# A two-layer encoder trunk on one core: expert weights in units of 2048 columns, and a finer alternation of large and small experts

## The chip, the core and the metric

The kernel runs on one core of a Trainium2 chip. The metric is the device time of one execution in microseconds; the median of three runs before the change is 1777.73 us (1777.11 to 1779.68). The engines are TensorE (PE; its weight loads are PEld), VectorE (DVE), ScalarE (ACT), GpSimd (POOL) and SyncE (SP), which issues the DMAs. Each works through its own queue in order.

## The reference

Two layers over 256 tokens of width 1024, all in float32. Each layer runs four token mixers (stick-breaking attention, spatial gating, chunk-band attention, an SSD scan) on one combined input projection, merges them by sigmoid gates, projects, and normalises. Then comes the channel sublayer, a dense SwiGLU in layer 0 and eight experts in layer 1, plus a gated per-layer embedding, and another normalisation:

```python
def swiglu(x, w_gate, w_up, w_down):
    return (jax.nn.silu(x @ w_gate) * (x @ w_up)) @ w_down
...
    top_val, top_idx = lax.top_k(logits, TOP_K)          # 2 of 8 experts a token
    gates = jax.nn.softmax(top_val, axis=-1)
...
    for e in range(N_EXPERTS):
        y = y + combine[..., e:e + 1] * swiglu(x, w_gate[e], w_up[e], w_down[e])
```

An expert has three matrices of 1024 x 3584 float32, 44 MB; all eight are read, 352 MB.

## The kernel before, in words

Weights and activations are used as pairs, `hi` (rounded to the matmul format F32R) and `lo` (the rest). `load` brings one weight unit of 128 rows x 1024 columns (512 KB, 4 KB rows) from HBM into a raw buffer; `split` makes `hi` by a ScalarE cast (L117) and `lo` by a VectorE subtraction (L118). `tmm` (L202) multiplies three passes: hi x hi, x.lo x hi, x.hi x lo, one matmul of 512 columns each.

The expert stage (`moe`) begins with the lead expert, number 7, whose weights need no routing result; the other seven follow in the order of their token counts, at places 1 to 7, their numbers read into registers of SP (L1200). Places 0 to 4 are large (class `Expert`, 128 token slots), places 5 to 7 small (class `Small`, 64 slots). An expert's 3584 inner columns go in seven chunks of 512. A chunk takes four units of gate weights, four of up and four of down: `proj(c, 0)`, `proj(c, 1)`, `turn(c)` (transposes of the hidden chunk on TensorE, into `pht` or `phs`, and a split of the result, `et` or `es`), `down(c)`. A unit costs a large expert six matmuls. A small expert puts hi and lo of its 64 slots side by side as 128 columns of the stationary operand (`passes`, L1057): four matmuls a unit, the upper 64 rows of the result holding the lo share. These halves are added afterwards: ScalarE copies the upper half to `st` (L1075), VectorE adds (L1082 for gate, L1092 for up), then comes the product (L1093).

`steps` (L1205 to L1214) writes the order by hand: three chunks of the first large expert, then the other 32 large chunks with 21 small chunks spread among them, chunk by chunk. Within a step the next chunk's gate projection, this chunk's turn, the next chunk's up projection and this chunk's down projection follow. Small work (SiLU, copies, products, splits) is `Delayed` by a number of loads, `D_SILU`, `D_MULT`, `D_TURN` = 3, 1, 1, and put behind that load's `hi` or `lo` on its engine. Gathers of token rows and the combination of an expert's result with the output are `tasks`, of which `tick` runs one piece after each unit.

Buffers: raw units rotate over 5 + 3 + 8 places, `hi` over five, `lo` over four. PSUM has three `stream` banks (projections, gathers, combines) and five `acc` banks (turns and down sums). While layer 1's embedding gate runs, ten units of the lead expert are loaded ahead (L1343 to L1350).

Of the kernel before, what the change touches and what calls it, by code (L numbers as in the profile page):

```python
# [17 lines left out]
P = 128  # L18
# [7 lines left out]
NE = 8  # L26
# [18 lines left out]
MLATE, MRAW = 3, 11  # L45
SK, TAIL = 4, 7
D_SILU, D_MULT, D_TURN = 3, 1, 1
# [3 lines left out]
ALONE = 3  # L51
# [47 lines left out]
def trunk_kernel(ctx: ExitStack, tc: tile.TileContext, a: dict, out: bass.AP):  # L99
# [5 lines left out]
    ring = ctx.enter_context(tc.tile_pool(name="ring", bufs=1))  # L105
    base = ctx.enter_context(tc.tile_pool(name="base", bufs=2))
    psum = ctx.enter_context(tc.tile_pool(name="psum", bufs=1, space=PSUM))

    def pst(name):
        return psum.tile([P, 512], F32, tag="stream", name=name, bufs=3)  # L110

    def psa(name):
        return psum.tile([P, 512], F32, tag="acc", name=name, bufs=5)
# [7 lines left out]
    spare = []  # L121
    count = [0]

    def raw_unit():

        i = count[0] % (RAW + MRAW)
        count[0] += 1
        if spare and i >= RAW:
            if i >= RAW + MLATE:
                return spare[1].tile([P, UN], F32, tag="mraw", name="mraw", bufs=MRAW - MLATE)  # L130
            return spare[0].tile([P, UN], F32, tag="mraw", name="mraw", bufs=MLATE)
        return ring.tile([P, UW], F32, tag="raw", name="raw", bufs=RAW)

    def load(src, n=UN, keep=None):
# [6 lines left out]
        if keep is None:  # L141
# [103 lines left out]
    sel(tris, -1, -1, 1, 0.0)  # L245
    iota = const.tile([P, P], F32, name="iota")
# [695 lines left out]
    class Weights:  # L942


        def __init__(self, e):
# [5 lines left out]
            self.proj = [[[m[c, i] for i in range(4)] for c in range(NCH)] for m in (g, u)]  # L951
            self.down = [d[k] for k in range(FE // P)]

        def first(self, n):

            g, u = self.proj
            return (g[0] + u[0] + g[1] + u[1] + self.down[0:4] + g[2] + u[2] + self.down[4:8])[:n]

    class Expert:
# [26 lines left out]
        def turn(self, c):  # L986
            self.mult.pop(c)()
            h, ps = self.h.pop(c), psa("pht")
# [13 lines left out]
        def down(self, c):  # L1002
            self.turned()
            if c == 0:
                self.acc = [psa("pey0"), psa("pey1")]
            for j in range(FC // P):
                k = c * (FC // P) + j
                w = load(self.w.down[k])
                x = self.hT[:, j * P : (j + 1) * P]
                ends = k == 0, k == FE // P - 1  # L1010
                tmm(*[(self.acc[h], w[:, h * 512 : (h + 1) * 512], x, *ends) for h in range(2)])
                self.tick()
# [39 lines left out]
    class Small(Expert):  # L1052
# [11 lines left out]
        def proj(self, c, which):  # L1064
            ps = pst("ps" + "gu"[which])
            for u in range(4):
                w = load(self.w.proj[which][c][u]).view("p (k c) -> p k c", k=2)
                ks = 2 * u, 2 * u + 1
                self.passes([(ps, w[:, k % 2, :], self.xg[:, k, :], k == 0, k == KD - 1) for k in ks])
                self.tick()  # L1070
            new = lambda n: self.fp.tile([HS, FC], F32, tag=n, name=n)
            t = new("st")

            def bring():
                after(nc.scalar.copy(t, ps[HS:P, :]), 0)  # L1075

            bring = Delayed(D_MULT, bring)
            if which == 0:
                self.h[c] = g = new("sg")

                def add():
                    after(nc.vector.tensor_tensor(g, ps[0:HS, :], t, op=ALU.add), 1)  # L1082

                add = Delayed(D_MULT + 1, add)
                silu = Delayed(D_SILU, lambda: after(act(g, g, AF.Silu), 0))
                self.silu = lambda: (bring(), add(), silu())
            else:
# [3 lines left out]
                def mult():  # L1091
                    nc.vector.tensor_tensor(t, ps[0:HS, :], t, op=ALU.add)  # L1092
                    nc.vector.tensor_tensor(g, g, t, op=ALU.mult)  # L1093

                mult = Delayed(D_MULT + 1, mult)
                self.mult[c] = lambda: (bring(), mult())

        def turn(self, c):
            self.mult.pop(c)()
            h, ps = self.h.pop(c), psa("phs")  # L1100
            n = FC // P
            for j in range(n):
                nc.tensor.transpose(ps[:, j * HS : (j + 1) * HS], h[:, j * P : (j + 1) * P], ident[:HS, :HS])
# [11 lines left out]
        def down(self, c):  # L1115
            self.turned()
            if c == 0:
                self.acc = [psa("pes0"), psa("pes1")]
            for j in range(FC // P):
                k = c * (FC // P) + j  # L1120
                w = load(self.w.down[k])
                ends = k == 0, k == FE // P - 1
                self.passes([(self.acc[h], w[:, h * 512 : (h + 1) * 512], self.hT[:, j, :], *ends) for h in range(2)])
# [9 lines left out]
    def moe(l, x, xt, fp, ep, route, lead, placed, first, second):  # L1133
# [71 lines left out]
        big = [(p, c) for p in range(BIG) for c in range(NCH)]  # L1205
        small = [(p, c) for p in range(BIG, NE) for c in range(NCH)]
        steps, big = big[:ALONE], big[ALONE:]
        nb, ns = len(big), len(small)
        done = 0
        for i, b in enumerate(big):  # L1210
            steps.append(b)
            while done < (i + 1) * ns // nb:
                steps.append(small[done])
                done += 1  # L1214
        ex = {}

        def expert(p):
            if p not in ex:
                w = lead if p == 0 else Weights(ids[p])
                ex[p] = (Expert if p < BIG else Small)(w, xgs[p], fp, ep, tick)  # L1220
            return ex[p]

        held.extend([None] * 3 + placed * 3)
        expert(0).proj(0, 0)
        tasks.append(prepare_small())
        expert(0).proj(0, 1)
        for n, (p, c) in enumerate(steps):
            if (p, c) == (0, 2):
                route.gates()
            if (p, c) == (0, 4):  # L1230
                list(second)
                tasks.append(prepare_pair(1))
            if (p, c) == (1, 1):
                tasks.append(prepare_pair(3))
            nxt = steps[n + 1] if n + 1 < len(steps) else None
            if nxt:
                expert(nxt[0]).proj(nxt[1], 0)
            ex[p].turn(c)
            if nxt:
                ex[nxt[0]].proj(nxt[1], 1)  # L1240
            ex[p].down(c)
            if c == NCH - 1:
                e = ex.pop(p)
                rank, sel_ = route.rank_at[:, :, p], route.sel_at[:, :, p]
                choice = lambda e=e, r=rank, s=sel_, o=chosen.pop(p, None): e.choice(r, s, o)
                tasks.append(e.combine(choice, route.gate_at[:, :, p], x, nxt is None))
# [26 lines left out]
    for l in range(DEPTH):  # L1273
# [57 lines left out]
        mixctx.close()  # L1331

# [228 lines left out]
```

## Time and profile before

| | |
|---|---|
| median of 3 runs | 1777.73 us |
| profiled execution, its own time | 1778.45 us |
| its span, first to last instruction | 1776.4 us |
| TensorE / VectorE / ScalarE busy | 1698.3 / 1402.4 / 1165.8 us |
| HBM read | 486 MB, 274 GB/s over the span |

Times in a profile are counted from the first instruction. Busy times of different stages are added up in the page, so a stage is read from a window of its own. A matmul's end is modelled, and it is drawn longer than the distance to the next one; the distance between starts is what it costs. A wait is put down to the engine that ended last before it.

### The profile page before, as it was taken

How to read it: one execution, taken by the hardware profiler on the slowest of the kernel's cores; microseconds unless marked ns; L12 is line 12 of the kernel's file. 1: busy time of each engine (PE TensorE's matmuls, PEld its weight loads, DVE VectorE, ACT ScalarE, POOL GpSimd, SP SyncE). 2: the span in 40 equal slices, each digit the busy share in tenths (PEclk: the TensorE clock that was granted, in tenths of full speed). 3: DMA queues.
4: the chain of work that ended last, by engine and by line, in shares of the span. 5: the costliest groups of instructions: out<-in, count | busy, mean ns of one | idle time of the engine just before them, and what ended most of it. 6: DMA issues, size and time to landing. Idle time of an engine off the chain costs nothing.

```text
span 1776.4 us, 27784 instructions
## 1 busy us (share of the span) xinstructions
PE 1698.3 (96%) x9476; PEld 1375.4 (77%) x9476; DVE 1402.4 (79%) x1645; ACT 1165.8 (66%) x1493; POOL 59.8 (3%) x129
## 2 busy tenths in 40 slices
PE   8999999999999999999999999999999999999995
PEld 8989998999899899878776766666666676667663
DVE  7646577455685475879899899999889899999997
ACT  6466445444455564468787878777777777777783
POOL 1000000000010000131000000000000000000001
PEclk9999999999999999999999999999999999999998
DMA  8633566566655358549899999999999999999991
GB/s 296 207 100 118 185 202 212 188 189 181 199 183 154 96 187 275 185 181 351 316 378 359 357 366 380 359 337 370 368 381 338 378 373 352 362 359 372 376 377 73
DMA packets 135862, 489.39 MB, mean 275 GB/s; under 512 B 15392, under 2 KB 15648, under 8 KB 135712
## 3 DMA queue, kind: packets, MB, share of 16 engines
q1 hardware_dynamic: 135712, 487.54, 76.9%
q8 instruction: 76, 1.25, 0.3%
q14 instruction: 74, 0.61, 0.1%
HBM read 486.43 MB, written 1.05 MB: 274 GB/s over the span
## 4 chain that ended last, share of the span: by engine, by line
PE 76%; DVE 9%; DMA 6%; ACT 4%; issue 3%; POOL 2%; DVEq 0%; SPq 0%; ACTq 0%; POOLq 0%
DVE lo L118 6%; PE pey L209 4%; PE peu L209 4%; PE peu L205 4%; PE peu L207 4%; PE peg L209 3%; PE pg L200 3%; PE pg L198 3%; PE pg L197 3%; PE peg L205 3%; PE peg L207 3%; ACT hi L117 3%; PE pey L205 3%; PE pey L207 3%; PE pes L1062 2%
## 5 line engine op out<-in xcount | busy, mean ns | idle before, releaser
L118 DVE TENSOR_TENSOR lo<-raw,hi 128x1024 fp32r<-128x1024 f32 (+1 forms) x444 | 529.4, 1211 | 181.0 <-PE pg L200 75.6
L117 ACT CAST hi<-raw 128x1024 fp32r<-128x1024 f32 (+1 forms) x444 | 455.0, 1044 | 265.3 <-PE pgu L198 49.7
L118 DVE TENSOR_TENSOR lo<-mraw,hi 128x1024 fp32r<-128x1024 f32 x464 | 543.4, 1216 | 23.8 <-ACT hi L117 17.3
L117 ACT CAST hi<-mraw 128x1024 fp32r<-128x1024 f32 x464 | 465.2, 1049 | 44.1 <-PE pey L207 13.6
L197 PE MATMUL pg<-xhi,hi 128*128 128x256 f32 x512 | 125.9, 283 | 0.1
L198 PE MATMUL pg<-xlo,hi 128*128 128x256 f32 x512 | 125.6, 283 | 0.0
L198 PEld LDWEIGHTS pg<-xlo,hi 128*128 128x128 f32 x512 | 97.0, 189 | 1.3 <-issue 1.3
L197 PEld LDWEIGHTS pg<-xhi,hi 128*128 128x128 f32 x512 | 97.0, 189 | 0.5 <-ACT t L697 0.5
L209 PE MATMUL pey<-lo,et 128*128 128x512 f32 x280 | 92.3, 411 | 3.5 <-DVE lo L118 2.6
L205 PE MATMUL pey<-hi,et 128*128 128x512 f32 x280 | 90.1, 402 | 5.8 <-ACT hi L117 5.4
L209 PE MATMUL peg<-lo,xghi 128*128 128x512 f32 x280 | 88.7, 398 | 0.3 <-DVE lo L118 0.2
L205 PE MATMUL peu<-hi,xghi 128*128 128x512 f32 x280 | 88.7, 396 | 0.0
L205 PE MATMUL peg<-hi,xghi 128*128 128x512 f32 x280 | 88.4, 395 | 0.0
L207 PE MATMUL peg<-hi,xglo 128*128 128x512 f32 x280 | 88.0, 393 | 0.0
L207 PE MATMUL pey<-hi,et 128*128 128x512 f32 x280 | 88.0, 395 | 0.0
L209 PE MATMUL peu<-lo,xghi 128*128 128x512 f32 x280 | 87.6, 394 | 0.3 <-DVE lo L118 0.3
L207 PE MATMUL peu<-hi,xglo 128*128 128x512 f32 x280 | 87.4, 393 | 0.0
L198 PE MATMUL pgu<-xlo,hi 128*128 128x256 f32 x352 | 85.9, 282 | 0.0
L197 PE MATMUL pgu<-xhi,hi 128*128 128x256 f32 x352 | 85.8, 282 | 0.0
L200 PE MATMUL pg<-xhi,lo 128*128 128x256 f32 x512 | 78.5, 287 | 0.0
L1062 PE MATMUL psu<-lo,xs 128*64 128x512 f32 x168 | 55.9, 414 | 19.0 <-DVE lo L118 19.0
L205 PEld LDWEIGHTS pey<-hi,et 128*128 128x128 f32 x280 | 50.9, 188 | 25.0 <-ACT hi L117 12.8
(374 smaller groups left out, 3200.0 us busy)
## 6 DMA issues: line engine op xcount, KB each, us to landing
mraw<-in_moe_down SPq DMA_DIRECT2D x156, 512.0 KB, 5.7
mraw<-in_moe_up SPq DMA_DIRECT2D x154, 512.0 KB, 5.8
mraw<-in_moe_gate SPq DMA_DIRECT2D x152, 512.0 KB, 5.3
raw<-in_w_feat SPq DMA_DIRECT2D x104, 512.0 KB, 3.6
raw<-in_moe_gate SPq DMA_DIRECT2D x70, 512.0 KB, 5.3
raw<-in_moe_up SPq DMA_DIRECT2D x70, 512.0 KB, 5.8
raw<-in_moe_down SPq DMA_DIRECT2D x68, 512.0 KB, 6.2
raw<-in_ffn_gate SPq DMA_DIRECT2D x22, 512.0 KB, 3.6
```

What stands on the lines that cost most here:

```text
L117: i = nc.scalar.copy(hi, src)
L118: return i, nc.vector.tensor_tensor(lo, src, hi.bitcast(F32), op=ALU.subtract)
L197: mm(o, w.hi, x.hi, start=first, stop=False, skip_group_check=True)
L198: mm(o, w.hi, x.lo, start=False, stop=False, skip_group_check=True)
L200: mm(o, w.lo, x.hi, start=False, stop=last, skip_group_check=True)
L205: mm(o, x.hi, w.hi, start=first, stop=False, skip_group_check=True)
L207: mm(o, x.lo, w.hi, start=False, stop=False, skip_group_check=True)
L209: mm(o, x.hi, w.lo, start=False, stop=last, skip_group_check=True)
L1062: mm(o[0:HS, :], x[:, 0:HS], w.lo, start=False, stop=last, skip_group_check=True)
```

## The change

Expert units are 2048 columns wide: 1 MB with 8 KB rows, two per projection and two per down chunk, with the HBM layout changed to match (also that of the embedding gate and projection). The narrow ring is closed before layer 1's channel sublayer, and a wide one opened (7 raw, 3 `hi`, 3 `lo`). Large and small experts are two generators that yield after each two units; nine steps of the large ones come first. A small expert's SiLU result is written to both halves of 128 rows, the up result is multiplied unfolded, and the turning matmul uses `ident2`, two 64-column identities on top of each other, so that it adds the halves. PSUM becomes four `stream` banks, two for large and two for small down sums; turns use `stream`. The lead expert's ahead loads are seven wide units, three before the router's and four behind.

```diff
-MLATE, MRAW = 3, 11
+WU = 2048
+WRAW, WLATE, WHI, WLO = 6, 1, 3, 3
 SK, TAIL = 4, 7
-D_SILU, D_MULT, D_TURN = 3, 1, 1
+D_SILU, D_MULT, D_TURN = 2, 2, 1
 LEAD = NE - 1
 BIG = 5
 HS = P // 2
-ALONE = 3
+ALONE = 9
...
+        return psum[0].tile([P, 512], F32, tag="stream", name=name, bufs=few[0])
+
+    def psa(name, tag="acc"):
+        return psum[0].tile([P, 512], F32, tag=tag, name=name, bufs=many[0])
+
+    def other_banks():
+
+        psumctx.close()
+        psum[0] = psumctx.enter_context(tc.tile_pool(name="psume", bufs=1, space=PSUM, reuse_waits="tile"))
+        few[0], many[0] = 4, 2
...
+        return wide_ring[i >= WRAW].tile([P, WU], F32, tag="wraw", name="wraw", bufs=(WRAW, WLATE)[i >= WRAW])
+
+    def begin_load(src):
+
+        raw = raw_unit()
+        nc.sync.dma_start(raw[:, : src.shape[-1]], src)
+        ahead.append((src, raw))
...
+        elif wide_ring:
+            hi = wide_ring[1].tile([P, WU], F32R, tag="hi", name="whi", bufs=WHI)
+            lo = wide_ring[1].tile([P, WU], F32R, tag="lo", name="wlo", bufs=WLO)
...
+    ident2 = const.tile([P, HS], F32, name="ident2")
+    nc.vector.tensor_tensor(ident2, ident[:, 0:HS], ident[:, HS:P], op=ALU.add)
...
-            for u in range(4):
-                w = load(self.w.proj[which][c][u]).view("p (k c) -> p k c", k=2)
-                ks = 2 * u, 2 * u + 1
-                tmm(*[(ps, w[:, k % 2, :], self.xg[:, k, :], k == 0, k == KD - 1) for k in ks])
+            for u in range(2):
+                w = load(self.w.proj[which][c][u], WU).view("p (k c) -> p k c", k=4)
+                ks = range(4 * u, 4 * u + 4)
+                tmm(*[(ps, w[:, k % 4, :], self.xg[:, k, :], k == 0, k == KD - 1) for k in ks])
...
-                self.h[c] = g = new("sg")
-
-                def add():
-                    after(nc.vector.tensor_tensor(g, ps[0:HS, :], t, op=ALU.add), 1)
-
-                add = Delayed(D_MULT + 1, add)
-                silu = Delayed(D_SILU, lambda: after(act(g, g, AF.Silu), 0))
+                g = self.fp.tile([P, FC], F32, tag="sg", name="sg")
+                t = self.fp.tile([HS, FC], F32, tag="st", name="st")
+                self.h[c] = g
+
+                def silu():
+                    for h in (slice(HS, P), slice(0, HS)):
+                        after(act(g[h, :], t, AF.Silu), 0)
+
+                bring = Delayed(D_MULT, lambda: after(nc.scalar.copy(t, ps[HS:P, :]), 0))
+                add = Delayed(
+                    D_MULT + 1, lambda: after(nc.vector.tensor_tensor(t, ps[0:HS, :], t, op=ALU.add), 1)
+                )
+                silu = Delayed(D_SILU + 2, silu)
                 self.silu = lambda: (bring(), add(), silu())
             else:
                 self.silu()
                 g = self.h[c]
 
-                def mult():
-                    nc.vector.tensor_tensor(t, ps[0:HS, :], t, op=ALU.add)
-                    nc.vector.tensor_tensor(g, g, t, op=ALU.mult)
-
-                mult = Delayed(D_MULT + 1, mult)
-                self.mult[c] = lambda: (bring(), mult())
+                self.mult[c] = Delayed(
+                    D_MULT, lambda: after(nc.vector.tensor_tensor(g, g, ps, op=ALU.mult), 1)
+                )
 
         def turn(self, c):
             self.mult.pop(c)()
-            h, ps = self.h.pop(c), psa("phs")
+            h, ps = self.h.pop(c), pst("phs")
             n = FC // P
             for j in range(n):
-                nc.tensor.transpose(ps[:, j * HS : (j + 1) * HS], h[:, j * P : (j + 1) * P], ident[:HS, :HS])
+                m1(ps[:, j * HS : (j + 1) * HS], h[:, j * P : (j + 1) * P], ident2)
...
+            for which in range(2):
+                expert(places[0]).proj(0, which)
+                yield
+            for n, (p, c) in enumerate(steps):
+                if (p, c) == (0, 2):
+                    route.gates()
+                if (p, c) == (0, 4):
+                    list(second)
+                    tasks.append(prepare_pair(1))
+                if (p, c) == (1, 1):
+                    tasks.append(prepare_pair(3))
+                nxt = steps[n + 1] if n + 1 < len(steps) else None
+                if nxt:
+                    expert(nxt[0]).proj(nxt[1], 0)
+                    yield
...
+                ex[p].turn(c)
+                if nxt:
+                    ex[nxt[0]].proj(nxt[1], 1)
+                    yield
+                ex[p].down(c)
...
+        held.extend([None] + placed * 2)
+        tasks.append(prepare_small())
+        big, small = run(range(BIG)), run(range(BIG, NE))
+        nb, ns = BIG * NCH * 3 - ALONE - 3, (NE - BIG) * NCH * 3
+        for i in range(ALONE):
+            next(big)
         done = 0
-        for i, b in enumerate(big):
-            steps.append(b)
+        for i in range(nb):
+            next(big)
             while done < (i + 1) * ns // nb:
-                steps.append(small[done])
+                next(small)
                 done += 1
-        ex = {}
-
-        def expert(p):
-            if p not in ex:
-                w = lead if p == 0 else Weights(ids[p])
-                ex[p] = (Expert if p < BIG else Small)(w, xgs[p], fp, ep, tick)
-            return ex[p]
-
-        held.extend([None] * 3 + placed * 3)
-        expert(0).proj(0, 0)
-        tasks.append(prepare_small())
-        expert(0).proj(0, 1)
-        for n, (p, c) in enumerate(steps):
-            if (p, c) == (0, 2):
-                route.gates()
-            if (p, c) == (0, 4):
-                list(second)
-                tasks.append(prepare_pair(1))
-            if (p, c) == (1, 1):
-                tasks.append(prepare_pair(3))
-            nxt = steps[n + 1] if n + 1 < len(steps) else None
-            if nxt:
-                expert(nxt[0]).proj(nxt[1], 0)
-            ex[p].turn(c)
-            if nxt:
-                ex[nxt[0]].proj(nxt[1], 1)
-            ex[p].down(c)
-            if c == NCH - 1:
-                e = ex.pop(p)
-                rank, sel_ = route.rank_at[:, :, p], route.sel_at[:, :, p]
-                choice = lambda e=e, r=rank, s=sel_, o=chosen.pop(p, None): e.choice(r, s, o)
-                tasks.append(e.combine(choice, route.gate_at[:, :, p], x, nxt is None))
+        for _ in big:
+            pass
+        list(small)
...
+        if l % 2:
+            ringctx.close()
...
+                pT = load(src_p, 2 * SEQ, into=two(2 * SEQ, ("oh", 3), ("oh", 3)))
+                pws = load(a["ple_proj"][l], WU, into=two(WU, ("xtlo", 1), ("xs", 1)))
+                pws = [pws[:, k * D : (k + 1) * D] for k in range(2)]
...
+                lead = Weights(LEAD)
+                srcs = lead.first(WRAW + WLATE)
+                for src in srcs[:3]:
+                    begin_load(src)
                 route = Route(l, xT, fp)
+                for src in srcs[3:]:
+                    begin_load(src)
```

## Rows read from the trace of the kernel before

**Rows 1.** the page: busy time, share of the span and instructions of each engine
```profile
PE 1698.3 (96%) x9476; PEld 1375.4 (77%) x9476; DVE 1402.4 (79%) x1645; ACT 1165.8 (66%) x1493; POOL 59.8 (3%) x129
```

**Rows 2.** busy time of each engine in two stretches (window, length, engines, clock, DMA)
```profile
775.00:870.00 95.00, 94.42 (x433) 76.81 (x432) 81.14 (x92) 71.96 (x80) 11.32 (x18) 1.00 0.89 326
870.00:1740.00 870.00, 825.57 (x3480) 584.53 (x3478) 802.25 (x792) 679.65 (x784) 0.00 (x0) 1.00 0.97 363
```

**Rows 3.** waits from 870 to 1740 us (who waited for whom, total, times, longest)
```profile
ACT st L1075 <- PE psg L1062: 50.9, 18, 3.7
PEld psu L1062 <- DVE lo L118: 45.3, 64, 1.0
PE psu L1062 <- DVE lo L118: 18.4, 35, 0.6
ACT hi L117 <- DMA mraw<-in_moe_up: 0.8, 1, 0.8
```

**Rows 4.** instruction groups, 870 to 1740 us (shapes, count, busy, mean, idle before)
```profile
L118 DVE TENSOR_TENSOR lo<-mraw,hi 128x1024 fp32r<-128x1024 f32 x418 | 487.9, 1215 | 19.7 <-ACT hi L117 16.8 <-PE pgt L209 1.5 <-PE peu L209 0.7
L117 ACT CAST hi<-mraw 128x1024 fp32r<-128x1024 f32 x417 | 416.2, 1049 | 27.2 <-PE pey L207 11.1 <-PE peu L207 3.5 <-PE peg L207 1.9
L118 DVE TENSOR_TENSOR lo<-raw,hi 128x1024 fp32r<-128x1024 f32 x186 | 218.4, 1214 | 7.4 <-ACT hi L117 6.5 <-PE peg L209 0.2 <-PE peu L209 0.2
L118 DVE TENSOR_TENSOR et<-pht,et 128x512 fp32r<-128x512 f32 x31 | 21.1, 681 | 0.0
L990 PE MATMUL pht<-ident,eh 128*128 128x128 f32 x124 | 18.8, 273 | 0.2
L117 ACT CAST et<-pht 128x512 fp32r<-128x512 f32 x31 | 18.1, 582 | 0.3 <-PE pht L990 0.3
L1093 DVE TENSOR_TENSOR sg<-sg,st 64x512 f32<-64x512 f32 x20 | 13.5, 677 | 0.0
L1103 PE MATMUL phs<-ident,sg 64*128 64x64 f32 x80 | 9.2, 235 | 0.0
L117 ACT CAST es<-phs 128x256 fp32r<-128x256 f32 x20 | 7.5, 374 | 1.8 <-PE phs L1103 1.5
L212 PE MATMUL pga<-oh,xthi 128*128 128x256 f32 x32 | 5.5, 284 | 0.8 <-ACT pg L91 0.8
```

**Rows 5.** matmuls in order of time, large expert (start, length, engine, line, operands, count)
```profile
1083.10 0.63 PE L205 MATMUL peu<-hi,xghi 128*128 128x512 f32 x2
...
1087.77 0.63 PE L207 MATMUL pey<-hi,et 128*128 128x512 f32 x2
1088.24 0.60 PE L990 MATMUL pht<-ident,eh 128*128 128x128 f32 x4
...
1088.59 0.71 PE L209 MATMUL pey<-lo,et 128*128 128x512 f32 x2
```

**Rows 6.** the same view a little later, from large into small expert
```profile
1092.63 0.57 ACT L117 CAST et<-pht 128x512 fp32r<-128x512 f32 x1
...
1097.41 0.73 PE L1060 MATMUL psu<-hi,xs 128*128 128x512 f32 x2 [0.69 <-ACT hi L117]
...
1098.67 0.68 PE L1062 MATMUL psu<-lo,xs 128*64 128x512 f32 x2 [0.52 <-DVE lo L118]
```

**Rows 7.** VectorE in order of time, eight of its passes in a row
```profile
1727.42 9.16 DVE L118 TENSOR_TENSOR lo<-mraw,hi 128x1024 fp32r<-128x1024 f32 x8
```

**Rows 8.** as rows 2, 25 microseconds within the stretch
```profile
910.00:935.00 25.00, 25.00 (x113) 19.19 (x111) 24.06 (x25) 22.25 (x27) 0.00 (x0) 1.00 1.02 409
```

**Rows 9.** DMA issues of one kind (count, size, median us from issue to landing)
```profile
mraw<-in_moe_up SPq DMA_DIRECT2D x154, 512.0 KB, 5.8
```

**Rows 10.** a full-precision F32 matmul group before 775 us, columns as in rows 4
```profile
L212 PE MATMUL pyd<-e,s 128*64 128x128 f32 x32 | 6.1, 273 | 0.0
```

**Rows 11.** end of the second output projection, ScalarE
```profile
738.40 1.05 ACT L117 CAST hi<-raw 128x1024 fp32r<-128x1024 f32 x1 [2.75 <-PE pwo L207]
```

**Rows 12.** end of the second output projection, TensorE
```profile
742.37 0.62 PE L209 MATMUL pwo<-lo,mhi 128*128 128x512 f32 x2
```

More of the change, by code (lines that the diff above doesn't have):

```diff
@@ L140, in load @@
             nc.sync.dma_start(raw[:, :n], src)
-        if keep is None:
+        if into is not None:
+            hi, lo = into
+        elif wide_ring:
+            hi = wide_ring[1].tile([P, WU], F32R, tag="hi", name="whi", bufs=WHI)
+            lo = wide_ring[1].tile([P, WU], F32R, tag="lo", name="wlo", bufs=WLO)
+        elif keep is None:
             hi = ring.tile([P, UW], F32R, tag="hi", name="hi", bufs=RHI)
@@ L987, in turn @@
             self.mult.pop(c)()
[L988 removed]
+            h, ps = self.h.pop(c), pst("pht")
             for j in range(FC // P):
@@ L1004, in down @@
             if c == 0:
[L1005 to L1011, printed above, removed]
+                self.acc = [psa("pey0", "accb"), psa("pey1", "accb")]
+            for u in range(2):
+                w, items = load(self.w.down[2 * c + u], WU), []
+                for i in range(2):
+                    j = 2 * u + i
+                    x = self.hT[:, j * P : (j + 1) * P]
+                    ends = c + j == 0, c == NCH - 1 and j == 3
+                    for h in range(2):
+                        s = i * D + h * 512
+                        items.append((self.acc[h], w[:, s : s + 512], x, *ends))
+                tmm(*items)
                 self.tick()
@@ L1117, in down @@
             if c == 0:
[L1118 to L1123, printed above, removed]
+                self.acc = [psa("pes0", "accs"), psa("pes1", "accs")]
+            for u in range(2):
+                w, items = load(self.w.down[2 * c + u], WU), []
+                for i in range(2):
+                    j = 2 * u + i
+                    ends = c + j == 0, c == NCH - 1 and j == 3
+                    for h in range(2):
+                        s = i * D + h * 512
+                        items.append((self.acc[h], w[:, s : s + 512], self.hT[:, j, :], *ends))
+                self.passes(items)
                 self.tick()
@@ L1204, in moe, with run, expert @@
         ]
[L1205 to L1208, printed above, removed]
+        other_banks()
+        def run(places):
+            steps = [(p, c) for p in places for c in range(NCH)]
+            ex = {}
+            def expert(p):
+                if p not in ex:
+                    w = lead if p == 0 else Weights(ids[p])
+                    ex[p] = (Expert if p < BIG else Small)(w, xgs[p], fp, ep, tick)
+                return ex[p]
+            for which in range(2):
[18 more added lines that the diff above has]
+                ex[p].down(c)
+                if c == NCH - 1:
+                    e = ex.pop(p)
+                    rank, sel_ = route.rank_at[:, :, p], route.sel_at[:, :, p]
+                    choice = lambda e=e, r=rank, s=sel_, o=chosen.pop(p, None): e.choice(r, s, o)
+                    tasks.append(e.combine(choice, route.gate_at[:, :, p], x, p == BIG - 1))
+                yield
@@ L1396, in gated @@
                 if apart:
-                    for u in range(4):
+                    for u in range(n):
                         unit(1, u)
```

94 lines of the change are left out of this document (41 added, 53 removed).

## The prediction

> **What bounds the kernel now.** I read the stages first, then the waits in the longest one, then the cadence of single engines. The page's totals (TensorE 96%, VectorE 79% busy [rows 1]) mix stages with different limits. The expert stage runs from 775 us, its first matmul, to about 1756. Up to 870 only large experts run; from 870 to 1740 large and small chunks alternate, and there the question is decided [rows 2]: TensorE 826 us of 870 busy, VectorE 802, DMA share 0.97 at 363 GB/s. Three engines look full, so each has to be worked out.
>
> TensorE. Its busy time flatters it: a matmul is drawn 0.39 us long while the next starts far earlier. Twenty matmuls start between 1083.10 and 1087.77 [rows 5], 4.67/20 = 0.2335 us each. The stretch has 3480 matmuls; without 124 + 80 transposes and 64 gathers (two groups of 32) [rows 2, 4] that is 3212 x 0.2335 = 750 us. Four large transposes take 1088.59 - 1088.24 = 0.35 us [rows 5], 0.0875 each, so 204 take 18; the gathers have half the columns, 64 x 0.117 = 7.5 (estimate from 0.2335). Sum 776. So 94 us of the 870 are stall.
>
> VectorE makes the low half of each weight unit, the pass `lo`: eight in a row take 9.16 us [rows 7], (9.16 - 1.215)/7 = 1.135 each, 604 of them [rows 4] 686 us. The other 116 of its 802 us are turns, products, folds and combines.
>
> The two don't stall evenly. A unit of 1024 columns costs TensorE 6 x 0.2335 = 1.40 us in a large expert, where `lo` (1.135) keeps ahead, but 4 x 0.2335 = 0.93 in a small one, where it can't. A small chunk is twelve such units: TensorE 11.2 + 0.35 us, VectorE 13.6 + 1.8 (three folding or product passes at 0.677 - 0.08 = 0.60) + about 0.33 for the turned half, 15.8 in all. The difference, 4.2 us, is not covered by four `lo` buffers; 94 us over the 20 small chunks in the stretch is 4.7 each. The waits say the same: TensorE's loads and matmuls of `psu` wait for `lo` (45.3 and 18.4 us), and ScalarE stands 50.9 us in front of the copy `st`, which waits for the last `psg` matmul while the next `hi` casts are queued behind it [rows 3]; TensorE then loses 0.69 and 0.52 us at once [rows 6].
>
> DMA is not it, although its share is 0.97: ScalarE's casts wait for weights once for 0.8 us [rows 3], and for 25 us it carried 409 GB/s [rows 8]. The stretch's 363 x 870 us = 316 MB would take 772 us at that rate.
>
> **The change, part by part.** Only layer 1 from its embedding gate on changes in kind.
>
> Wide units. 604 `lo` passes become 302 of 2048 columns. No row has that length; from 512 to 1024 columns a pass grows from 681 to 1215 ns [rows 4], 1.043 ns a column, so 2048 take 1.215 + 1.068 = 2.283 us, and 2.203 in a row (0.08 overlap as now), against 2 x 1.135 = 2.270. That is 302 x 0.067 = 20 us off VectorE. Bounds: none of it, or one whole fixed part of 0.147 (1.215 - 1.068) per merged pair, 44 us. I take 20, because it is the difference that the cadence shows. The `hi` cast grows likewise from 1.049 to 1.049 + (1.049 - 0.582) x 2 = 1.98 us; ScalarE stays at most 680 of 870 us [rows 2].
>
> Small up-fold. One of the three VectorE passes per small chunk and one ScalarE copy go; 20 x 0.60 = 12 us off VectorE. ScalarE gains a second SiLU call in the place of the copy, at about the same length. The fold is now done by the turning matmul, a full-precision product with 64 columns on 128 rows instead of a transpose. The nearest row is a full-precision product of 128 columns, 6.1/32 = 0.19 us [rows 10]; the present transpose is at 0.0875. Over 84 matmuls that is between 0 and 84 x 0.10 = 9 us; half the columns lies near 0.10, so +1.
>
> Finer alternation. A step is now two wide units: large, TensorE 24 x 0.2335 + 0.12 = 5.72 us, VectorE 2 x 2.203 + 0.40 = 4.81; small, TensorE 16 x 0.2335 + 0.13 = 3.87, VectorE 4.41 + 0.51 = 4.92. VectorE loses 1.05 us in a small step and regains 0.91 in each large one, of which there are 93 to 63, 1.48: 1.35 back for 1.05 lost. Three wide buffers hold over 5 us of small work. So the shortage that made 4.7 us of stall per small chunk is spread to where it is covered. The delays of `st` and the sums are now two or three wide loads, so ScalarE meets a finished `psg` instead of waiting for it.
>
> What is late next. The demands on the stretch become TensorE 777, VectorE 802 - 32 = 770, DMA 772: all alike, none with room to cover for another. I therefore don't take the whole 94 us. Remaining are combines and gathers that push in between (their PSUM banks now rotate with the projections' and the turns' over four, so one may wait for a SiLU that stands behind a 1.98 us cast), and dips of the DMA, which has to run near its best rate. I take half, -47 us (823 us, TensorE at 94%). Bounds: 0, and -84 (TensorE at 777 + about 10).
>
> DMA. Half as many, 1 MB each, seven buffers for sixteen of half the size (14 against 16 units). A buffer now takes 5.8 us from issue to landing [rows 9] and then a cast and a pass; with a doubled time in flight, 11.6 + 1.98 + 2.28 = 16 us, under 7 x 2.6 = 18 at the forecast rate. Cost nothing; if that cover goes, a unit is late by the difference, at most 2 us in 18. The rate of 8 KB rows stands in no row: bounds 409 GB/s as now and, downwards, the 363 of the stretch (a rival below).
>
> Start and end. The embedding gate's units now sit where the narrow ring was, whose last reader is the output projection ending at 743.0 [rows 12]; before, the cast began at 738.4 [rows 11]. Two wide `lo` (4.6 us) may fall into the layer norm on VectorE: between -2 and +5, taken +2, since the transposed rows are waited for there anyway. The lead expert's first 7 MB are issued behind those gate loads and the router on SP, ahead of the register loads of the expert ids; 3 MB need no release. The last three large steps run alone, at TensorE's cadence; 0, between -3 and +3.
>
> Sum, against the profiled execution's own 1778.45 us (span 1776.4 and 2 around): -47 + 1 + 2 = 1734.5. The median of the runs is 0.7 lower, so **1734**.
>
> **Rivals.**
> B: the DMA is full now. Its share is 0.97, and 363 GB/s may be all it sustains; then nothing that engines save counts, and the time stays at 1778. For it: the share. Against: 409 GB/s over 25 us [rows 8], and no cast waits for weights [rows 3]. The Trainium skill states such a limit, DMA: Bandwidth & Descriptors, section Bandwidth: some 358 GB/s of HBM per core bind a load. By that rule the stage could not shrink at all; the trace disagrees with it for this single core, by 363 over 870 us and 409 over 25.
>
> C: everything fits. With three wide buffers TensorE stalls hardly at all: 777 + 10 = 787, -83 + 3, **1698**. For it: VectorE's balance of 1.35 to 1.05. Against: three engines within 1% of each other.
>
> D: the turn stands in the line, slower. The cast of the turned half follows the first wide cast on ScalarE and holds the next one. Counted from the end of the small transposes, 0.37 + 1.98 + 2.28 = 4.63 us until the next `lo` is there, while TensorE has one wide unit and the first half of the next, 1.87 + 0.93 = 2.80: 1.83 us exposed, and with the 1.05 that VectorE is behind, 2.88, times 21 chunks 60 us. Large: 0.58 + 1.98 + 2.28 = 4.84 against 2.80 + 1.87 = 4.67, times 35 another 6. Together 66: **1800**. It decides from about 2.1 us exposed per small chunk (44/21). Against: now the transposes run at 1088.24 and their cast only at 1092.63 [rows 5, 6], and ScalarE waits 0.3 and 1.8 us in all for them [rows 4], so they are done early.
>
> **How the numbers follow.** My forecast (a quarter to three quarters of the stall gone, 1712 to 1757) 0.60; C 0.17; B 0.09; D 0.14. A measurement of this kernel can't tell less than 0.2%, 3.6 us, from no change. Forecast and C are faster: 0.77; B the same: 0.09; D slower: 0.14. The range goes from C's 1698 less the 44 - 20 us that `lo` might bring if only a quarter of it counted, 1692, to just past B, 1779.
>
> **What would show it.** `lo` near 2.28 us and 336 times in the expert stage; TensorE's waits for `lo` down from 64 us to under 35; the wait of `st` for `psg` near zero; DMA from 363 to about 384 GB/s over the alternating stretch. B is right if casts wait for DMA; D, if casts of the turned half wait and TensorE idles just behind small transposes. I am wrong if the gain comes before 775 us, or if `lo` costs more than 2.43 us (twice 1.215), since then VectorE is the bound again.

## The result, and the profile after

The changed kernel takes **1749.85 us** (median of 4 runs, 1749.47 to 1750.35) where the kernel before took 1778.7 in the same comparison: ratio 0.9837, 95% interval [0.9822, 0.9851]. That is 28.9 us less; 44 were forecast. The number lies within the range and within the likeliest case's own 1712 to 1757. The main reason given for it did not stand, as the experiments show, so that the number came out is in part luck.

The page of the changed kernel, busy time by engine; it answers to [rows 1].

```profile
PE 1677.9 (96%) x9560; PEld 1402.3 (80%) x9560; DVE 1360.8 (78%) x1284; ACT 1130.8 (65%) x1152; POOL 61.1 (3%) x129
```

VectorE has 361 instructions fewer. TensorE has 84 more: the small turning product counts as two instructions each. The profiled span is 1747.3 us against 1776.4. Three cuts place the 29.1 us. The first expert matmul starts at 778.15, before at 775.06, so the start costs 3.1. The last weight pass ends at 1725.91 + 1.07 = 1726.98, before at 1755.84 + 0.68 = 1756.52; what follows it takes 20.3 against 19.9. So the expert stage went from 981.4 to 948.8 us, **32.6 less where 47 were forecast**. The rows of these times, first and last matmuls over expert weights, in the kernel before and then in the changed one:

```profile
775.06 0.67 PE L205 MATMUL peg<-hi,xghi 128*128 128x512 f32 x2
...
1755.84 0.68 PE L1062 MATMUL pes<-lo,es 128*64 128x512 f32 x2 [0.19 <-DVE lo L118]
```

```profile
778.15 1.19 PE L223 MATMUL peg<-whi,xghi 128*128 128x512 f32 x4 [0.67 <-ACT xglo L955]
...
1725.91 1.07 PE L227 MATMUL pey<-wlo,et 128*128 128x512 f32 x4
```

The window that is used for every kernel with wide units below, here of the changed kernel, columns as in [rows 2]:

```profile
844.00:1700.00 856.00, 819.07 (x3623) 620.91 (x3623) 776.70 (x478) 658.47 (x486) 0.00 (x0) 0.99 0.96 375
```

375 GB/s where 363 stood and 384 were forecast: the weights come 3% faster. The waits of that window (who waited for whom, total us, times, longest); the line of `st` and the two of `psu` answer to [rows 3].

```profile
ACT sg L92 <- PE phs L230: 30.0, 9, 4.1
...
ACT eh L92 <- PE pht L1010: 19.7, 9, 3.6
ACT st L1104 <- PE psg L1086: 16.8, 14, 2.8
ACT eh L92 <- PE peg L227: 13.8, 10, 2.3
...
DVE wlo L127 <- ACT whi L126: 57.5, 52, 3.4
...
PEld psu L1086 <- DVE wlo L127: 22.9, 22, 1.6
...
PE psu L1086 <- DVE wlo L127: 14.0, 20, 1.1
```

TensorE's waits for the low half in `psu` fell from 64 to 36.9 us, and `st` waits 16.8 us in the place of 50.9. But VectorE now waits 57.5 us for casts (16.8 + 6.5 = 23.3 before [rows 4]), and two waits are new: ScalarE stands 30.0 and 19.7 us in front of a SiLU, for the turn of the chunk *before*, which still reads the one buffer that the SiLU writes. Groups of the same window (count, busy us, mean ns, idle before), to set against [rows 4]:

```profile
L127 DVE TENSOR_TENSOR wlo<-wraw,whi 128x2048 fp32r<-128x2048 f32 x307 | 689.6, 2287 | 57.7 <-ACT whi L126 57.5
L126 ACT CAST whi<-wraw 128x2048 fp32r<-128x2048 f32 x306 | 575.3, 1913 | 60.3 <-PE pey L225 24.0 <-PE peg L225 13.1 <-PE peu L225 6.8
```

The wide pass is 2287 ns, forecast 2283. VectorE's busy time over the run fell by 1402.4 - 1360.8 = 41.6 us, and yet it waits.

### The profile page after: what moved, and what is told of

Its sections match the earlier page's. It is cut to its first block, busy times and chain, and to the rows that moved or that the text cites. A ratio compares the mean times of both kernels' runs of the same rounds, so it can differ in the third digit from the quotient of the medians.

```text
span 1747.3 us, 24927 instructions
## 1 busy us (share of the span) xinstructions
PE 1677.9 (96%) x9560; PEld 1402.3 (80%) x9560; DVE 1360.8 (78%) x1284; ACT 1130.8 (65%) x1152; POOL 61.1 (3%) x129
## 3 DMA queue, kind: packets, MB, share of 16 engines
HBM read 486.43 MB, written 1.05 MB: 279 GB/s over the span
## 5 line engine op out<-in xcount | busy, mean ns | idle before, releaser
L127 DVE TENSOR_TENSOR wlo<-wraw,whi 128x2048 fp32r<-128x2048 f32 x340 | 764.7, 2287 | 67.0 <-ACT whi L126 66.8
L126 ACT CAST whi<-wraw 128x2048 fp32r<-128x2048 f32 x340 | 640.0, 1913 | 83.5 <-PE pey L225 26.9
L127 DVE TENSOR_TENSOR lo<-raw,hi 128x1024 fp32r<-128x1024 f32 (+2 forms) x227 | 274.5, 1212 | 167.0 <-PE pg L218 75.8
L126 ACT CAST hi<-raw 128x1024 fp32r<-128x1024 f32 (+2 forms) x227 | 236.1, 1041 | 237.9 <-PE pgu L216 50.8
L227 PE MATMUL peg<-wlo,xghi 128*128 128x512 f32 x280 | 78.9, 403 | 0.0
L223 PE MATMUL peg<-whi,xghi 128*128 128x512 f32 x280 | 78.2, 402 | 0.7 <-ACT xglo L955 0.7
L227 PE MATMUL pey<-wlo,et 128*128 128x512 f32 x280 | 77.5, 398 | 1.2 <-DVE wlo L127 1.2
L223 PE MATMUL peu<-whi,xghi 128*128 128x512 f32 x280 | 77.4, 398 | 0.7 <-ACT pg L92 0.7
L227 PE MATMUL peu<-wlo,xghi 128*128 128x512 f32 x280 | 77.8, 399 | 0.2 <-DVE wlo L127 0.2
L223 PE MATMUL pey<-whi,et 128*128 128x512 f32 x280 | 76.1, 392 | 1.7 <-ACT whi L126 1.7
L225 PE MATMUL pey<-whi,et 128*128 128x512 f32 x280 | 75.2, 390 | 0.0
```

What stands on the lines that cost most here:

```text
L126: i = nc.scalar.copy(hi, src)
L127: return i, nc.vector.tensor_tensor(lo, src, hi.bitcast(F32), op=ALU.subtract)
L223: mm(o, x.hi, w.hi, start=first, stop=False, skip_group_check=True)
L225: mm(o, x.lo, w.hi, start=False, stop=False, skip_group_check=True)
L227: mm(o, x.hi, w.lo, start=False, stop=last, skip_group_check=True)
```

## Experiments

All medians are of 4 to 10 runs; the kernel before gave 1777.6 to 1778.3 beside them, and the interval is that of the ratio to it.

### Is it the finer alternation?

Changed kernel, one yield per chunk in the place of three:

```diff
-ALONE = 9
+ALONE = 3
...
                 if nxt:
                     expert(nxt[0]).proj(nxt[1], 0)
-                    yield
...
                     ex[nxt[0]].proj(nxt[1], 1)
-                    yield
...
-        nb, ns = BIG * NCH * 3 - ALONE - 3, (NE - BIG) * NCH * 3
+        nb, ns = BIG * NCH - ALONE, (NE - BIG) * NCH
```

> The changed kernel with one thing undone: the two generators yield once per chunk (six wide units) instead of every two units. Theory A (the finer alternation covers VectorE's shortage in small experts): most of the 29 us gain goes, 1768 to 1778 us, and the waits of TensorE for the lo pass, 38 us on psu and pes loads now, go to 80 or more. Rival B (the gain is VectorE's saved work, 32 us by the forecast's sum): at most 8 us are lost, 1750 to 1758.

Measured: **1743.48**, [0.9793, 0.9825]. The coarse order is 6 us *faster* than the fine one, which neither expectation allowed. The forecast's main step is refuted as the source of this kernel's gain. Yet TensorE does wait as that step says, now in the down products of small experts (waits of this kernel, 844 to 1700 us):

```profile
PEld pes L1086 <- DVE wlo L127: 45.3, 37, 1.8
```

### Is it the wide passes, or the large transfers?

Changed kernel, cast and pass in halves of 1024 columns, DMA still 1 MB; and, by itself, the DMA in two halves of 512 KB, passes wide:

```diff
-        last[:] = split(raw[:, :n], hi[:, :n], lo[:, :n])
+        for c in range(0, n, UN):
+            s = slice(c, min(c + UN, n))
+            last[:] = split(raw[:, s], hi[:, s], lo[:, s])
```

```diff
-        nc.sync.dma_start(raw[:, : src.shape[-1]], src)
+        for c in range(0, WU, UN):
+            nc.sync.dma_start(raw[:, c : c + UN], src[:, c : c + UN])
...
-            nc.sync.dma_start(raw[:, :n], src)
+            for c in range(0, n, UN if n == WU else n):
+                s = slice(c, c + (UN if n == WU else n))
+                nc.sync.dma_start(raw[:, s], src[:, s])
```

> The changed kernel with the cast and the lo pass of each wide unit issued as two of 1024 columns; the DMAs stay 1 MB. VectorE gets back 336 x (2 x 1.135 - 2.203) = 22 us of work, ScalarE a similar share. Rival B: it is paid nearly in full, 1765 to 1775. Theory A: VectorE has room where the alternation is fine, 1750 to 1758. A third possibility is a gain: with half-size passes a matmul could start earlier if the first half were waited for alone, 1740 to 1749.

> The changed kernel with each wide unit loaded by two DMAs of 512 KB, rows of 4 KB out of 8 KB. Rival C (8 KB rows make the DMA faster, and that is the gain): 1765 to 1778, and the mean rate in the alternating stretch falls from 372 to about 363 GB/s. Theories A and B: no change, 1748 to 1753.

Measured: narrow passes **1733.56**, [0.9732, 0.9765], 16 us faster than the change with wide ones and faster than any case that was expected, although they keep VectorE busy longer. Half-size transfers **1750.24**, [0.9832, 0.9865]: no difference. The wide pass saves VectorE about what was priced (over the whole run it is busy for 1360.8 us against 1386.2, 25 less; 20 were forecast), and the kernel loses 16 by it. The window of the kernel with narrow passes:

```profile
844.00:1700.00 856.00, 834.77 (x3700) 632.03 (x3699) 812.88 (x802) 698.40 (x811) 0.00 (x0) 1.00 0.97 381
```

VectorE is busy 36 us more in the same 856 us, and TensorE 16; part of the 36 is that this kernel gets further in the window (3700 matmuls against 3623). So VectorE's capacity was not the bound of the changed kernel.

### The fold

Changed kernel with the old small fold (sums of 64 rows, then transposes):

```diff
...
+                def mult():
+                    after(nc.vector.tensor_tensor(t, ps[0:HS, :], t, op=ALU.add), 1)
+                    nc.vector.tensor_tensor(g, g, t, op=ALU.mult)
...
-                m1(ps[:, j * HS : (j + 1) * HS], h[:, j * P : (j + 1) * P], ident2)
+                nc.tensor.transpose(ps[:, j * HS : (j + 1) * HS], h[:, j * P : (j + 1) * P], ident[:HS, :HS])
...
```

> The changed kernel with the small experts' up-fold done as before: copy and sum for the up result too, SiLU once, transposes of 64 rows instead of the full-precision turning product. VectorE +21 x 0.60 = 13 us, TensorE: eight product instructions take 0.81 us per chunk now against about 0.37 for four transposes, so -21 x 0.44 = -9 us. If VectorE is the bound now: 1757 to 1765. If TensorE is: 1739 to 1747. If neither by itself: 1748 to 1755.

Measured: **1753.57**, [0.985, 0.9883]. The new fold brings 3.7 us, hardly more than the 3.6 that the prediction names as the least that can be told; taken as the saved VectorE and ScalarE work less a dearer product. A small turn in the kernel before and in the changed kernel, TensorE in order of time:

```profile
1140.70 0.46 PE L1103 MATMUL phs<-ident,sg 64*128 64x64 f32 x4
1141.09 0.73 PE L209 MATMUL pey<-lo,et 128*128 128x512 f32 x2
```

```profile
1141.26 1.00 PE L230 MATMUL phs<-ident,sg 128*128 128x64 f32 x8
1142.07 1.18 PE L227 MATMUL peg<-wlo,xghi 128*128 128x512 f32 x4
```

It is 1142.07 - 1141.26 = 0.81 us where four small transposes took 1141.09 - 1140.70 = 0.39: over 21 chunks 8.8 us, at the upper bound of 9 and not the +1 taken. One product takes 0.81 / 4 = 0.20 us, as much as the 0.19 of one with 128 columns [rows 10] and not half of it.

### Both orders with both widths

```diff
# the edits of the chunkwise run and of the narrow passes together
```

> The changed kernel with both alternatives that were faster than it: order chunk by chunk, and passes of 1024 columns on 1 MB DMAs. If the two gains (6 and 16 us) come from different waits they add up: 1726 to 1730. If both only shorten the same chain cast, lo pass, matmul: 1732 to 1738. Theory A, that the fine order is needed once VectorE has 22 us more work to do, says slower than with narrow passes alone: 1738 to 1750.

Measured: **1742.05**, [0.9782, 0.9814], within the 1738 to 1750 that was expected if the fine order is needed once VectorE has the narrow passes' work. The four runs:

| | wide passes | narrow passes |
|---|---|---|
| fine order | 1749.85 | 1733.56 |
| chunkwise | 1743.48 | 1742.05 |

The fine order is worth 8.5 us with narrow passes and costs 6.4 with wide ones; the wide passes cost 16 in the fine order and 1 in the coarse. The effects don't add, and none of the four explains how 1778 became 1742 in the kernel that has neither. The edits left are buffers and delays.

### Buffers or delays, in the kernel before

Three runs start from the kernel *before*: only more `hi` and `lo` buffers (with 13 raw units in the place of 16, to make room); only later delays, `D_SILU` 5 and `D_MULT` 3, which is roughly what 2 and 2 wide units mean; both.

```diff
-RAW, RHI, RLO = 5, 5, 4
-MLATE, MRAW = 3, 11
+RAW, RHI, RLO = 5, 6, 6
+MLATE, MRAW = 3, 8
```

```diff
-D_SILU, D_MULT, D_TURN = 3, 1, 1
+D_SILU, D_MULT, D_TURN = 5, 3, 1
```

> The kernel before with one part alone: six hi and six lo buffers of 1024 columns instead of five and four, as many columns as the wide ring holds (13 raw units instead of 16 pay for them). Theory D (the gain is the longer lookahead in prepared weights): 1750 to 1764. Theory E (the gain is that small work is placed later in the queues): 1773 to 1778.

> The kernel before with one part alone: small work placed later, D_SILU, D_MULT from 3, 1 to 5, 3 loads of 1024 columns. The wait of the copy st for psg, 51 us on ScalarE, should go. Theory E: 1752 to 1766. Theory D: 1772 to 1779, since with four lo buffers VectorE can't be further ahead than before.

> The kernel before with both, six hi and lo buffers and the later placing. If buffers and placing are the whole of the change's good half, this comes to the changed kernel with narrow passes and chunkwise order, less the saved fold (4 us) and with 512 KB DMAs, which cost nothing: 1730 to 1745. If narrow raw buffers, PSUM banks or the larger groups of matmuls count as well: 1750 to 1765.

Measured: buffers **1777.91**, [0.9992, 1.0011]: nothing. Delays **1731.96**, [0.9722, 0.9754]: 45.6 us from one line, more than the whole change brings and more than either expectation allowed. Both **1730.92**, [0.9716, 0.9748]. What happens is seen on ScalarE in order of time. The kernel before:

```profile
1125.53 0.58 ACT L117 CAST et<-pht 128x512 fp32r<-128x512 f32 x1
1129.78 0.58 ACT L1075 COPY st<-psg 64x512 f32<-64x512 f32 x1 [3.68 <-PE psg L1062]
1130.27 2.94 ACT L117 CAST hi<-mraw 128x1024 fp32r<-128x1024 f32 x3
```

and the same kernel with later delays:

```profile
922.61 4.84 ACT L117 CAST hi<-mraw 128x1024 fp32r<-128x1024 f32 x5 [0.35 <-PE pey L207]
927.36 0.58 ACT L117 CAST et<-pht 128x512 fp32r<-128x512 f32 x1
927.96 0.58 ACT L1075 COPY st<-psg 64x512 f32<-64x512 f32 x1
```

In the first, ScalarE stands 3.68 us in front of the copy until the projection's last matmul is done, then three casts follow in a row: they had only been queued behind it. In the second the copy stands behind more casts and waits for nothing. What the 3.68 us do to the others, in the kernel before:

```profile
1131.34 1.23 DVE L118 TENSOR_TENSOR lo<-mraw,hi 128x1024 fp32r<-128x1024 f32 x1 [0.60 <-ACT hi L117]
```

```profile
1131.36 0.73 PE L1060 MATMUL psu<-hi,xs 128*128 128x512 f32 x2 [0.49 <-ACT hi L117]
1132.62 0.69 PE L1062 MATMUL psu<-lo,xs 128*64 128x512 f32 x2 [0.53 <-DVE lo L118]
...
1134.35 0.67 PE L1062 MATMUL psu<-lo,xs 128*64 128x512 f32 x2 [0.57 <-DVE lo L118]
```

VectorE waits 0.60 us for a cast, TensorE 0.49 for a cast and then 0.53 for the pass that this made late; the 0.57 is for the next pass, which on VectorE stands behind the sum `sg` as well. Rows like the last two are those from which the prediction read that VectorE can't keep ahead [rows 6]. That ScalarE doesn't take a later cast past a waiting copy agrees with the Trainium skill, TensorE: Matmul & The Clock Gate, section "Architectural detail: the array is 16× 32×32, not 1× 128×128", by which ScalarE and VectorE work their queues strictly first in, first out.

How long it stands can be worked out. With B `hi` buffers, the cast of the d-th unit behind a projection can be issued once TensorE has freed the unit B places ahead of it, so the copy behind that cast comes up to B - d units too early (roughly: the cast's own 1.05 us is left out). A narrow small unit is 4 x 0.2335 = 0.93 us: before, 5 - 1 = 4 units are 3.7 us (longest wait of `st` for `psg`: 3.7); with later delays 5 - 3 = 2 are 1.9 (longest 1.8). The two runs with six buffers bear it out: 6 - 1 = 5 units are 4.7 us (longest 4.8), and with later delays 6 - 3 = 3 are 2.8 (longest 2.9). So more buffers alone make ScalarE stand longer, 61.1 us where it stood 44.6, which fits their gaining nothing; that kernel's wait from 870 to 1700 us:

```profile
ACT st L1075 <- PE psg L1062: 61.1, 17, 4.8
```

For the wide kernels the working is short: the changed kernel has 3 - 2 = 1 wide small unit, 8 x 0.2335 = 1.9 us, and a longest wait of 2.8.

Waits from 870 to 1700 us, kernel before and below it the kernel with later delays:

```profile
ACT eh L91 <- PE peg L209: 46.7, 22, 2.2
ACT st L1075 <- PE psg L1062: 44.6, 16, 3.7
ACT st L1075 <- PE psu L1062: 23.0, 16, 1.8
```

```profile
PEld psu L1062 <- DVE lo L118: 26.8, 46, 1.0
...
ACT st L1075 <- PE psg L1062: 16.8, 14, 1.8
...
ACT eh L91 <- PE peg L209: 15.1, 20, 0.8
```

VectorE stands in the same way. In the kernel before, in the same window, its longest wait in total is in front of the large product `eh`, which is queued before the up projection's last matmul is done; with later delays this row is gone:

```profile
DVE eh L984 <- PE peu L209: 30.4, 22, 1.6
```

So VectorE was held up both by late casts and at the head of its own queue. The two delays were moved together, and the runs don't tell ScalarE's standing from VectorE's.

The DMA of the kernel with later delays carries 380 GB/s in that window, where the kernel before has 363:

```profile
870.00:1700.00 830.00, 809.09 (x3498) 592.53 (x3496) 801.66 (x795) 681.50 (x788) 0.00 (x0) 1.00 0.99 380
```

### Which of the placings

The kernel before, later delays for small experts alone (`S_SILU` and `S_MULT` in class `Small` in the place of `D_SILU` and `D_MULT`):

```diff
+S_SILU, S_MULT = 5, 3
...
```

> Kernel before with the later placing for small experts alone (copies and sums 3 and 4 loads behind, SiLU 5), large ones as they were. Before, ScalarE waited 67.6 us for st (psg 44.6, psu 23.0) and 46.7 us for eh (peg) between 870 and 1700; placing all later gave 45.6 us. If each wait is worth the same, small alone gives 27 of these: 1751 (1746 to 1756). If only the small copies count (TensorE's stall was put down to small chunks): 1732 to 1738. If only the large SiLU counts: over 1768.

Measured: **1754.71**, [0.9852, 0.9885], 23.6 us of the 45.6. Its waits, 844 to 1700 us, show the half that is left:

```profile
ACT eh L92 <- PE peg L210: 39.8, 21, 2.7
...
DVE eh L985 <- PE peu L210: 25.3, 22, 1.4
```

So the large experts' SiLU (on ScalarE) and product (on VectorE) are worth about 22 us (45.6 - 23.6, if the two halves add up), although TensorE's waits show mostly in small chunks.

### The placing in the changed kernel, undone and carried on

Undone in part (copies, products and large SiLUs one wide load behind, sums two), and the opposite, SiLUs one wide load later, with wide and with narrow passes:

```diff
-D_SILU, D_MULT, D_TURN = 2, 2, 1
+D_SILU, D_MULT, D_TURN = 1, 1, 1
...
-                silu = Delayed(D_SILU + 2, silu)
+                silu = Delayed(4, silu)
```

```diff
-D_SILU, D_MULT, D_TURN = 2, 2, 1
+D_SILU, D_MULT, D_TURN = 3, 2, 1
```

> Changed kernel with the placing partly undone: copies, products and the large SiLUs one wide load behind their projection (as two narrow loads) and the sums two; the small SiLU stays at four loads. Theory E (it is the placing that gained): ScalarE's waits of st for psg (16.8 us) and of eh for peg (13.8) rise to over 60 together, and the time to 1757 to 1772. Theory A (the finer alternation and the wide units gained): 1747 to 1753, as placed work finds its operands ready either way.

> Changed kernel with the SiLUs one wide load later (D_SILU 3 in the place of 2: large 3 loads behind, small 5); nothing else. Theory F: the changed kernel still makes ScalarE stand, because a SiLU is queued before the turn of the chunk before has freed its one buffer: its waits of sg for phs (30.0 us) and of eh for pht (19.7 us) between 844 and 1700 are 50 us in which no cast is issued, and VectorE then waits 59 us for casts. One load later the turn lies ahead of the SiLU: both waits under 15 us together, VectorE's wait for casts under 40, time 1733 to 1742 (a quarter to a third of the 50 us comes back). Rival G: the wide chain itself (cast 1.91, then pass 2.29 us, over three buffers) is what costs, and ScalarE would only stand elsewhere: 1747 to 1752.

> Changed kernel with casts and passes of 1024 columns (1733.6 us as measured) and the SiLUs one wide load later. Theory F: here too ScalarE waits for the turn before, 24.5 us (eh for pht) and 14.7 (sg for phs); with these gone a quarter to a third of 39 us comes back: 1721 to 1726. Rival G: the narrow passes have already taken away what could be had, 1731 to 1736.

Measured: undone **1772.29**, [0.9954, 0.9977]: 22.4 of the 28.9 us are gone, with everything else of the change in place. Its waits, 844 to 1700 us:

```profile
DVE wlo L127 <- ACT whi L126: 83.4, 61, 4.1
ACT st L1104 <- PE psg L1086: 42.6, 16, 6.0
ACT eh L92 <- PE peg L227: 30.8, 13, 5.3
```

Later, wide passes: **1738.33**, [0.9755, 0.9787], 11.5 less than the change. Later, narrow passes: **1721.67**, [0.9667, 0.9699], 12 less than narrow passes alone, and the fastest of all kernels here, 1778.31 - 1721.67 = 56.6 us below the kernel before. Waits of the wide one:

```profile
DVE wlo L127 <- ACT whi L126: 46.2, 47, 4.1
...
ACT sg L92 <- PE phs L230: 20.4, 9, 3.1
```

Its wait of `eh` for `pht` is 9.6 us, so the two together fell from 49.7 to 30.0 only, not under 15, and VectorE's wait to 46, not under 40; the time came out in the middle of the expected range. The narrow one, group and window:

```profile
L127 DVE TENSOR_TENSOR wlo<-wraw,whi 128x1024 fp32r<-128x1024 f32 x631 | 729.3, 1215 | 20.0 <-ACT whi L126 18.8 <-PE psu L1088 0.7
```

```profile
844.00:1700.00 856.00, 839.24 (x3760) 644.39 (x3758) 823.48 (x814) 706.37 (x819) 0.00 (x0) 1.00 0.96 382
```

VectorE waits 18.8 us for casts and TensorE is busy for 839 of 856 us.

## Why the prediction was right, and where not

**The time.** 1749.85 against 1734. Start +3.1 against +2, tail +0.4 against 0: both held. The expert stage is the term that was off: -32.6 against "I take half, -47 us". It came near because the later delays, which had no price in the sum, gave back a part of the same stall; that is luck.

**The step that failed** is "Finer alternation": "So the shortage that made 4.7 us of stall per small chunk is spread to where it is covered." Spreading that shortage is not what gained. Without the fine alternation the changed kernel is faster (1743.5), and with 25 us more VectorE work it is faster too (1733.6). The stall of 94 us was seen rightly, and so was that no engine needed the whole time; about half of it, 45.6 us, goes with later placing alone, that is, with ScalarE and VectorE no longer standing in front of small operations whose operands aren't there, while casts and passes stand behind. The prediction had the row, 50.9 us of `st` [rows 3], and the two stalls at 1097 us [rows 6] directly behind such a wait (the copy at 1095.83 had stood 2.63 us), and it gave the later delays one sentence at the end of the same paragraph, without a price: "so ScalarE meets a finished `psg` instead of waiting for it". The placing for small experts, which that sentence names, is worth 23.6 us in the kernel before; the large experts' waits, 46.7 and 30.4 us of `eh`, it left out. The sum per small chunk, 15.8 us of VectorE against 11.5 of TensorE, came out at the 4.7 us of stall without being the whole of its cause: the large experts show it, where the pass "keeps ahead" and yet some 22 us were to be had.

That VectorE is slower than TensorE in a small chunk was read rightly. In the kernel before, TensorE starts the last pass of one small unit after the other at VectorE's distance of 1.13 us and not at its own 0.93:

```profile
1126.79 0.68 PE L1062 MATMUL psg<-lo,xs 128*64 128x512 f32 x2
...
1127.92 0.68 PE L1062 MATMUL psg<-lo,xs 128*64 128x512 f32 x2
```

How much of the other half of the 94 us this is, no run shows; with the later delays VectorE is busy for 801.7 of 830 us.

**Wide units.** Duration right (2.283 forecast, 2.287 measured), effect wrong: the 20 us off VectorE bring nothing, and in the fine order the wide pass costs 16. The cast was forecast at 1.98 us and takes 1.91. The runs show what goes with it, VectorE's wait for casts (57.5 us, without the later delays 83.4, with narrow passes and later SiLU 18.8). Whether that is the longer chain of cast, pass and matmuls over three coarse buffers, or short work queued behind a 2.29 us pass, was not separated.

**Fold.** +1 on TensorE's path was too little (8.8 us of TensorE time), and its relief outweighs it: -3.7 in all.

**DMA cost nothing**: held, with more room than the sum had: a 1 MB unit lands 6.8 to 7.2 us after its issue (medians of the changed kernel), not 11.6. (At the forecast 384 GB/s it is used up in 2.73 us and not in the prediction's 2.6, which changes nothing.) Transfers of 1 MB and 512 KB give the same time, and the rate follows the engines: 363, 375, 380, 382 GB/s. Rival B is out: no wait for a transfer is among those of the changed kernel, and the rate rose by a change of placing alone. The Trainium skill's DMA: Bandwidth & Descriptors, section "Bandwidth", asks for at least 1 MiB in a transfer; here, with several of 512 KB in flight, the step to 1 MB brought nothing (1750.24 against 1749.85).

**C and D.** C's 1698 was not reached by any kernel. D's mechanism exists, once: at 893.23 TensorE waits 2.88 us for the turned half `es`. Its cast stands on ScalarE behind a wide cast and then the SiLU in two parts, its low half on VectorE behind a wide pass; the rival had priced such a wait for every chunk. ScalarE and then VectorE there:

```profile
890.54 1.27 ACT L92 ACTIVATE sg<-st 64x512 f32<-64x512 f32 x2
891.84 0.37 ACT L126 CAST es<-phs 128x256 fp32r<-128x256 f32 x1
```

```profile
890.55 2.29 DVE L127 TENSOR_TENSOR wlo<-wraw,whi 128x2048 fp32r<-128x2048 f32 x1 [0.50 <-ACT whi L126]
892.76 0.42 DVE L127 TENSOR_TENSOR es<-phs,es 128x256 fp32r<-128x256 f32 x1
```

A relative of it was missed: the SiLU that waits for the turn before it, 49.7 us, 11.5 of them had back by one load of delay.

**Signs named beforehand.** `lo` time: right. TensorE's waits under 35: 36.9, just missed. `st` near zero: 16.8, missed; by the working above the copy still comes one wide load too early. 384 GB/s: 375. Their halfway values together said what the time says, that the stall was taken away in part.

**Open.** What makes the rest of the stall that the later delays leave, some 94 - 46 = 48 us. Why the fine order gains 8.5 us with narrow passes and loses 6.4 with wide ones; why the chunkwise kernel with narrow passes and the new fold (1742.05) is 10 us behind the kernel before with later delays (1731.96), though both order the work by chunks. Their buffers, banks and exact delays differ, and that was not tried apart.

## What to carry to other kernels

When an engine waits for a pass, follow the wait back to the engine that feeds the pass, and look at what stood at the head of *its* queue: a short operation on a fresh result, placed fewer units behind than the ring has buffers, holds back ready work for (buffers - delay) units each time. Place such operations nearer to as many units behind as there are buffers: the SiLUs of large experts were run at that delay (5 with five narrow buffers, 3 with three wide ones), copies and products only at 3 of 5 and 2 of 3, and every step later that was run gained. That one line was worth 45.6 us in the kernel before, more than the whole change, which held a part of the same placing. When a change rewrites units, its delays counted in units change too: price that by itself.

## What the runs showed of the hardware

The granted clock fell inside the expert stage, which it did not before. TensorE and then the window, in the changed kernel:

```profile
893.23 1.36 PE L1084 MATMUL psu<-whi,xs 128*128 128x512 f32 x4 [2.88 <-DVE es L127]
894.39 1.91 PE L1086 MATMUL psu<-wlo,xs 128*64 128x512 f32 x4
896.10 1.74 PE L1084 MATMUL psu<-whi,xs 128*128 128x512 f32 x4
```

```profile
894.00:898.00 4.00, 4.00 (x12) 2.56 (x11) 1.44 (x1) 2.02 (x2) 0.00 (x0) 0.57 0.75 277
```

After 2.88 us without a matmul the granted clock averages 0.57, so most of these 4 us are at the lower level of 1.2 GHz, and eight matmuls take 896.10 - 893.23 = 2.87 us where 8 x 0.2335 = 1.87 is the cadence: the wait of 2.88 us cost TensorE at least 1.0 us more behind it. Two other such dips, from 972 and from 1558 us, have 0.66 and 0.67 over 5 us. The chunkwise kernel with wide passes has 1.00 in the same three stretches, so a part of its 6.4 us may lie here; that was not tried.
